# Hybrid attention and DeltaNet layer: token sums from the high and low halves, one gate block earlier, later planned output weights

## The chip, the cores and the metric

The kernel runs on one core of one Trainium2 chip. The metric is the device time of one execution in microseconds (us); lower is better. The kernel before takes 763.55 us, the median of three executions between 762.99 and 765.27 us.

## The reference, cut to what matters

One decoder layer on 512 tokens and 16 meta tokens in front of them (528 columns), width 1024. The tokens are normalised once; two branches, softmax attention (8 heads, names `a*`) and a gated DeltaNet (8 heads, names `d*`), read the same normalised tokens `hn`:

```python
hn = rms_norm(h, norm_w)
proj = hn @ w_in                     # aq ak av az dq dk dv dz db da ga gd
y_a = (rms(o_a) * 0.8 * silu(az)) @ w_branch_attn
y_d = (rms(o_d) * silu(dz)) @ w_branch_delta
merged = sigmoid(ga) * y_a + sigmoid(gd) * y_d
out = rms_norm(h + merged @ w_out, final_norm_w)[:, 16:]
```

## The kernel before, in words

**Products.** Every weight block (128 output channels, 1024 inputs) is split into a high part `wh` (rounded, by an ACT copy) and a low part `wl` (the rest, by a DVE subtraction); the tokens likewise into `hnH` and `hnL`. A product is three passes, high by high, high by low, low by high, over 8 input blocks. The blocks come in the order that `dense_order` (L34) writes out: for each of four groups of two heads, `dk` and `dv` of both heads, then `dq`, `dz` and the attention blocks, then the gates and the two branch outputs.

**Pairs.** Some neighbouring blocks (from group 0: `ak` with `av`) are computed two at a time by seven half products instead of eight (`pair_of_blocks`, L1844, the products p1 to p7 in the order p1, p2, p6, p5, p7, p4, p3). p1 and p2 read `hnH` and `hnL` directly; p6, p5, p7 and p4 read four token sums t1 to t4: sums and differences of the quarters of `hn` (512 input channels by 264 tokens, so 128 x 1056 numbers each). With the quarters called A (first channels, first tokens), B (first channels, second tokens), C and E (second channels), the kernel needs t1 = B - A, t2 = E - t1, t3 = E - B and t4 = C - t2.

**Normalising.** `normalise` (L524) squares, scales and transposes a tile of 128 tokens through PE into a PSUM bank of the kind `pat`. `part` (L557) copies the bank to `hnH` on ACT, subtracts on DVE to `hnL`, and a third task, `whole` (L563), copies the unsplit numbers on ACT into `whole_`, four SBUF tiles that are the same memory as `room0` to `room3`. The bank is given back when both `hnL` and `whole` are through. There are 12 such ACT copies.

**The sums.** `token_sums` (L607) waits for the 12 copies and for the event `ap` (L828, the end of the chain of small decay operations of `gates`, L640), then forms the four sums, one DVE subtraction each; `high_low` (L611) splits each into `sumH` (ACT) and `sumL` (DVE). When all four are split, the two `th` buffers become free, which are halves of `room3` (L835).

**Gates.** `after_gate` (L911) takes the finished product of a `dz` or `az` block out of its PSUM bank: it waits for a `th` buffer, then runs a tanh on ACT and a multiplication on DVE, and only then gives the bank back. Banks of the kind `pd`, which all dense products use, are three (L66); a pair needs one for p1 and p6, one for p2, later others.

**What sets the order of work.** All instructions are laid out before the run by a planner (`Plan`). It resumes tasks one by one: of all tasks that wait for an engine it takes the one that can start earliest by its own cost estimates, and the lower rank where two could start at the same time. Ranks: 0 for loads, splits of weights and the DeltaNet, 0.6 for `gates`, 1 for what follows a product, 2 for attention, 3 for `token_sums`, 4 for the dense products. Each engine then runs its instructions in exactly that order, so one that waits holds all behind it. `Engine.time` (L235) holds the costs; a transfer is taken to land by `transfer` (L138):

```python
self.hwdge = max(begin + 600, self.hwdge) + 460
self.dma = max(self.dma, self.hwdge) + nbytes / 360 + 20
self.arrival = self.dma + 900
```

(nanoseconds and bytes; `late`, L134, adds to the arrival). Weights come through four `raw` buffers (`load_weights`, L476, all on SP's queue, in the order of the blocks) and are split by `split` (L401). The eight blocks of `w_out` follow the last weights; numbers 4 and 5 of them are split into free `W` buffers, the others into the memory of `hn` once that is free.

**The end.** In the last pair of the attention branch (`pair_products`, L1766) PE's products p1, p6 and p7 are each followed by a copy of their bank on ACT (`snap`, L1770, tile `sn`). p4 goes on accumulating in the bank that p7 left, so PE starts it only after the copy.

All instructions are issued through one helper, so the profile's line is L231 for nearly all; the tiles tell them apart.

Of the kernel before, what the change touches and what calls it, by code (L numbers as in the profile page):

```python
# [10 lines left out]
F32 = mybir.dt.float32  # L11
# [3 lines left out]
ALU = mybir.AluOpType  # L15
# [5 lines left out]
KB = D // P  # L21
# [12 lines left out]
def dense_order():  # L34

    order = []
    for g in range(H // 2):
        k, v, q, z = ([(n, 2 * g), (n, 2 * g + 1)] for n in ("dk", "dv", "dq", "dz"))
        a0, a1 = ([(n, 2 * g + i) for n in ("ak", "av", "aq", "az")] for i in range(2))
        order += k + v + (a0 + q + z[:1] if g else q + z[:1] + a0) + a1 + z[1:]  # L40
    order += [("gd", c) for c in range(KB)] + [("ga", 0)]
    for n in range(KB):
        order += [("ga", n + 1)] * (n < KB - 1) + [(("yd", "ya")[n // 4], 2 * (n % 4) + i) for i in range(2)]
    return order
# [17 lines left out]
HALF = L // 2  # L62
# [6 lines left out]
PE, DVE, ACT, POOL, SP = "PE", "DVE", "ACT", "POOL", "SP"  # L69
# [19 lines left out]
class Plan:  # L89
# [24 lines left out]
    def spawn(self, gen, rank=None):  # L114
        time, src = self.here() if self.task else (0.0, SP)
        self.tasks.append(Task(gen, self.task.rank if rank is None else rank, time, src))
# [99 lines left out]
class Engine:  # L216
# [18 lines left out]
    def time(self, op, args, kw):  # L235
        if op == "dma_start":
            return {SP: 60, ACT: 700, POOL: 1050}[self.name]
        out = kw["out"] if "out" in kw else args[0]
        ins = [a for a in list(args[1:]) + list(kw.values()) if hasattr(a, "dtype") and hasattr(a, "space")]
        n = int(np.prod(out.shape[1:]))  # L240
        if self.name == PE:
            if op == "transpose":
                return 2 * max(n / 2.4, 53)
            dt = ins[-1].dtype
            if dt == F32:
                small = ins[0].shape[0] <= 64
                return 2 * max(2 * n / 2.4 + 4, 32 if small else 107)
            if dt == F32R:
                return n / 2.4 + (11 if n < 400 else 18) if n >= 256 else max(2 * n / 2.4, 107)
            return n / 2.4 + 57  # L250
        psum = any(a.space == PSUM for a in ins)
        if op == "tensor_reduce":
            n = int(np.prod(ins[-1].shape[1:]))
        scalar = any(hasattr(kw.get(k), "space") for k in ("scalar", "scalar1", "scale", "bias"))
        if self.name == ACT:
            return (51 if op == "copy" and psum else 94) + n / 1.2 + 50 * scalar + 93 * ("accum_out" in kw)
        if self.name == DVE:
            one = op in ("tensor_copy", "tensor_scalar", "tensor_scalar_mul", "tensor_scalar_add", "memset")
            return 69 + 60 * (scalar or op == "scalar_tensor_tensor") + n / (1.92 if one and not psum else 0.96)
        if op == "tensor_tensor":  # L260
            return 300 + 164 * n if kw["op"] == ALU.pow else 100 + 2.2 * n
        return 100 + n / 1.1
# [3 lines left out]
def hybrid_block(ctx: ExitStack, tc: tile.TileContext, x, meta, wblk, wbd, wout, pcol, prow, out):  # L266
    nc = tc.nc
    plan = Plan({**SLOTS, "wo": 0, "th": 0}, BANKS, ALL_BANKS)
    T, V, A, G, S = (Engine(plan, n, e) for n, e in
                     ((PE, nc.tensor), (DVE, nc.vector), (ACT, nc.scalar), (POOL, nc.gpsimd), (SP, nc.sync)))  # L270
    spawn, done = plan.spawn, plan.done
# [29 lines left out]
    def give(kind, at=None):  # L301
        plan.give(kind, names_.index(at.tensor.name) if kind in BANKS else 0)
# [9 lines left out]
    def tick(event, n):  # L312
        ticks[event] = ticks.get(event, 0) + 1
        if ticks[event] == n:
            done(event)
        return ticks[event] == n
# [159 lines left out]
    def load_weights(n):  # L476
        yield ("raw",)
        which = plan.task.slot
        raw = raws[which]
        yield SP  # L480
        m = n - len(ORDER)
        S.dma_start(out=raw, in_=wblk[n] if m < 0 else wout[m // 4, :, m % 4 * D:m % 4 * D + D])
        if n in PAIRED or m < 0 and ORDER[n][0] in ("yd", "ya"):
            first.append((raw, which))
            if len(first) == 2:
                spawn(split_pair(n - 1, tuple(first)), 0)
                first.clear()
        else:
            spawn(split(n, raw, which), 0.3 if n < 2 else 0 if m < 0 else 2)
# [32 lines left out]
    hn = [hnp.tile([P, KB, L], F32R, tag=t, name=t) for t in ("hnH", "hnL")]  # L522

    def normalise(n):  # L524

        yield f"x{n}"
        w = P if n == 0 else D
        ss, rs, dg = (mk(sp, [P, k], F32, t, 3) for k, t in ((1, "ss"), (1, "rs"), (P, "dg")))
        yield ACT
        A.activation(out=st[:, :w], in_=xt[n], func=AF.Square, accum_out=ss)  # L530

        def weigh():
            yield "nwb"
            yield DVE
            V.tensor_tensor(out=xt[n], in0=xt[n], in1=mt[:, P:2 * P] if n == 0 else nwb, op=ALU.mult)
            done(f"xw{n}")

        spawn(weigh())
        src = ss
        if n == 0:  # L540
            yield "same"
            yield ("pdl",)
            yield PE
            pt = bank("pdl")
            T.matmul(pt[:, 0:1], samb.rearrange("p k t -> p (k t)"), ss, start=True, stop=True)
            src = pt[:, 0:1]
        yield DVE
        V.tensor_scalar(out=ss, in0=src, scalar1=1.0 / D, scalar2=EPS, op0=ALU.mult, op1=ALU.add)
        if n == 0:
            give("pdl", pt)  # L550
        yield POOL
        G.tensor_tensor(out=rs, in0=ss, in1=mhalf[:, 0:1], op=ALU.pow)
        yield DVE
        V.tensor_scalar_mul(out=dg, in0=ident, scalar1=rs)
        yield f"xw{n}"

        def part(pt, dst):  # L557
            yield ACT
            A.copy(out=hn[0][dst], in_=pt)
            tick(f"hh{n}", 1 if n == 0 else 2)  # L560
            bank_ = f"hn bank {n} {dst[1].start}"

            def whole():  # L563

                t0, t1 = dst[2].start, dst[2].stop
                for c in (0, KB // 2) if n == 0 else (dst[1].start,):
                    for m in range(2):
                        lo, hi = max(t0, HALF * m), min(t1, HALF * m + HALF)
                        if lo < hi:
                            yield ACT  # L570
                            A.copy(out=whole_[2 * (c // 4) + m][:, :, lo - HALF * m:hi - HALF * m],
                                   in_=pt[:, c - dst[1].start:c - dst[1].start + 4, lo - t0:hi - t0])
                if tick(bank_, 2):
                    give("pat", pt)
                tick("whole", 9)

            spawn(whole(), 0.6)
            yield DVE
            V.tensor_tensor(out=hn[1][dst], in0=pt, in1=hn[0][dst].bitcast(F32), op=ALU.subtract)
            if tick(bank_, 2):  # L580
                give("pat", pt)
            tick(f"hn{n}", 1 if n == 0 else 2)

        for hf in range(1 if n == 0 else 2):
            yield ("pat",)
            yield PE
            pt = bank("pat")
            if n == 0:
                T.matmul(pt[:, 0:P], xt[0], dg, start=True, stop=True)
                pt = pt[:, 0:P].rearrange("p (k t) -> p k t", t=NM)  # L590
                dst = (slice(None), slice(0, KB), slice(0, NM))
            else:
                pt = pt.rearrange("p (k t) -> p k t", t=P)
                for k in range(4):
                    T.matmul(pt[:, k, :], xt[n][:, (4 * hf + k) * P:(4 * hf + k + 1) * P], dg, start=True, stop=True)
                dst = (slice(None), slice(4 * hf, 4 * hf + 4), slice(NM + P * (n - 1), NM + P * n))
            spawn(part(pt, dst))
# [7 lines left out]
    of_sum = dict(t1=0, t2=3, t3=1, t4=2)  # L605

    def token_sums():  # L607
        yield "whole"
        yield "ap"

        def high_low(key):  # L611
            n = of_sum[key]
            yield ACT
            A.copy(out=ts_h[n], in_=whole_[n])
            yield DVE
            V.tensor_tensor(out=ts_l[n], in0=whole_[n], in1=ts_h[n].bitcast(F32), op=ALU.subtract)
            done(key)
            if tick("sums", 4):
                for n in range(SLOTS["th"]):
                    plan.give("th", n)  # L620

        for key, (x_, y_) in dict(t1=(1, 0), t3=(3, 1), t2=(3, 0), t4=(2, 3)).items():
            yield DVE
            V.tensor_tensor(out=whole_[of_sum[key]], in0=whole_[x_], in1=whole_[y_], op=ALU.subtract)
            spawn(high_low(key))


    FULL = [(0, 272), (272, 256)]
# [1576 lines left out]
```

## Time and profile before

| | |
|---|---|
| median of 3 executions | 763.55 us (762.99 to 765.27) |
| profiled execution, own time | 767.75 us |
| its span, first to last instruction | 766.0 us |
| PE (matmul) busy | 740.0 us, 97% of the span |
| DVE busy | 620.2 us, 81% |
| ACT busy | 500.4 us, 65% |
| POOL busy | 89.6 us, 12% |
| granted TensorE clock, mean | 0.989 of full speed |

PE is TensorE's matmuls, PEld its weight loads, DVE VectorE, ACT ScalarE, POOL GpSimd, SP the engine that issues the DMAs. A row of the timeline is start, duration (us), engine, operation, output <- inputs, shapes, count, and in brackets the engine's idle time before it and what ended it. PEclk is the granted TensorE clock as a share of full speed: 1.00 is 2.4 GHz, 0.50 is 1.2 GHz.

### The profile page before, as it was taken

To read this page: it belongs to the slowest core of one execution; us is meant where nothing else is said; L and a number is where in the kernel's file an instruction comes from. 1 tells how busy PE (TensorE), PEld (TensorE's weight loads), DVE (VectorE), ACT (ScalarE), POOL (GpSimd) and SP (SyncE) were. 2 spreads that over 40 slices of the span, in tenths; PEclk is the share of its full clock that TensorE was granted. 3 is DMA by queue.
4 is the path that set the end of the run, shared out by engine and by line. 5 is a ranking of instruction groups with operands and counts; after the bars stand their busy time and mean duration, and the time that the engine had idled before them with its cause. 6 is when DMAs were issued, how large, how long until landed. Compare 5 with 4: busy or idle time off the path is not lost.

```text
span 766.0 us, 14381 instructions
## 1 busy us (share of the span) xinstructions
PE 740.0 (97%) x5311; PEld 671.6 (88%) x5311; DVE 620.2 (81%) x1427; ACT 500.4 (65%) x1318; POOL 89.6 (12%) x102
## 2 busy tenths in 40 slices
PE   4999999999999999999999999999999999999996
PEld 4998888899999799999889989988888998898775
DVE  6799999699899659989877979975697879797353
ACT  6479576679865848986587977667776446454132
POOL 4134002112000201401020311000100000000001
PEclk9999999999999979999999999999999999999999
DMA  8031423224304103421320441360123442143502
GB/s 320 30 113 32 135 83 70 70 70 149 98 33 145 31 34 119 147 81 42 118 64 22 159 135 33 120 184 30 56 83 116 147 148 91 57 131 111 193 1 110
DMA packets 45430, 74.86 MB, mean 98 GB/s; under 512 B 20728, under 2 KB 25636, under 8 KB 45360
## 3 DMA queue, kind: packets, MB, share of 16 engines
q1 hardware_dynamic: 45360, 73.95, 30.0%
q8 instruction: 41, 0.67, 0.3%
q14 instruction: 29, 0.24, 0.1%
HBM read 67.58 MB, written 6.36 MB: 97 GB/s over the span
## 4 chain that ended last, share of the span: by engine, by line
PE 74%; DVE 10%; ACT 10%; issue 2%; DMA 1%; POOL 1%; SPq 0%; POOLq 0%; DVEq 0%; ACTq 0%
PE bank L231 71%; PE psc L231 3%; ACT wh L231 2%; DVE wl L231 2%; DVE y L231 1%; ACT TM L231 1%; DMA xt<-in_x_dram 1%; POOL km L231 1%; ACT ak L231 1%; ACT e L231 1%; DMA raw<-in_wout_dram 1%; ACT ktd L231 1%; DVE ak L231 1%; DVE ast L231 1%; ACT y L231 1%
## 5 line engine op out<-in xcount | busy, mean ns | idle before, releaser
L231 PE MATMUL bank<-hnH,wh 128*128 128x512 f32 (+4 forms) x664 | 233.6, 355 | 1.6 <-ACT hnH L231 1.3
L231 PE MATMUL bank<-hnL,wh 128*128 128x512 f32 (+4 forms) x664 | 222.0, 337 | 0.0
L231 PE MATMUL bank<-hnH,wl 128*128 128x512 f32 (+4 forms) x664 | 221.7, 337 | 0.0
L231 DVE TENSOR_TENSOR wl<-raw,wh 128x1024 fp32r<-128x1024 f32 (+1 forms) x120 | 134.4, 1121 | 20.2 <-ACT wh L231 19.6
L231 ACT CAST wh<-raw 128x1024 fp32r<-128x1024 f32 (+1 forms) x120 | 116.4, 970 | 48.6 <-PE bank L231 34.5
L231 PEld LDWEIGHTS bank<-hnH,wh 128*128 128x128 f32 x664 | 124.5, 189 | 14.5 <-ACT hnH L231 1.5
L231 PEld LDWEIGHTS bank<-hnH,wl 128*128 128x128 f32 x664 | 124.3, 189 | 14.0
L231 PEld LDWEIGHTS bank<-hnL,wh 128*128 128x128 f32 x664 | 124.5, 189 | 9.5
L231 PE MATMUL bank<-sumH,wh 128*128 128x264 f32 x224 | 68.0, 303 | 0.0
L231 PE MATMUL bank<-sumL,wh 128*128 128x264 f32 x224 | 63.9, 285 | 0.4 <-DVE sumL L231 0.4
L231 PE MATMUL bank<-sumH,wl 128*128 128x264 f32 x224 | 63.8, 285 | 0.0
L231 DVE SCALAR_TENSOR_TENSOR y<-xp,pc,y 128x528 f32<-128x528 f32 (+1 forms) x72 | 54.1, 757 | 0.5 <-ACT y L231 0.5
L231 ACT ACTIVATE e<-psc,ast 128x144 f32<-128x144 f32 (+3 forms) x64 | 34.7, 542 | 18.4 <-DVE ast L231 16.6
L231 PEld LDWEIGHTS bank<-sumL,wh 128*128 128x128 f32 x224 | 42.6, 190 | 0.6 <-DVE sumL L231 0.6
L231 PEld LDWEIGHTS bank<-sumH,wh 128*128 128x128 f32 x224 | 42.7, 190 | 0.2
L231 PEld LDWEIGHTS bank<-sumH,wl 128*128 128x128 f32 x224 | 42.4, 189 | 0.0
L231 PE MATMUL bank<-btH,wh 128*128 128x256 f32 x128 | 36.2, 283 | 2.1 <-ACT sn L231 2.1
L231 PE MATMUL bank<-btH,wl 128*128 128x256 f32 x128 | 36.0, 281 | 0.0
L231 PE MATMUL bank<-btL,wh 128*128 128x256 f32 x128 | 35.9, 281 | 0.0
L231 POOL TENSOR_TENSOR ass<-ass,mhalf 128x4 f32<-128x4 f32 x8 | 10.3, 1288 | 186.8 <-DVE ass L231 175.2
L231 PE MATMUL psc<-ak,aq 128*128 128x264 f32 (+3 forms) x160 | 29.1, 303 | 0.4 <-ACT e L231 0.3
L231 DVE TENSOR_REDUCE ast<-psc 128x1 f32<-128x528 f32 (+3 forms) x40 | 28.5, 714 | 0.5
(370 smaller groups left out, 1738.2 us busy)
## 6 DMA issues: line engine op xcount, KB each, us to landing
raw<-in_wblk_dram SPq DMA_DIRECT2D x96, 512.0 KB, 3.6
raw<-in_wout_dram SPq DMA_DIRECT2D x8, 512.0 KB, 4.9
xt<-in_x_dram SPq DMA_DIRECT2D x4, 512.0 KB, 6.4
TM<-gcd SPq DMA_DIRECT2D x8, 256.0 KB, 5.9
xr<-in_x_dram SPq DMA_DIRECT2D x8, 256.0 KB, 6.0
out_dram<-xr SPq DMA_DIRECT2D x8, 256.0 KB, 2.1
room<-scrm SPq DMA_DIRECT2D x12, 128.0 KB, 3.5
oad<-room SPq DMA_DIRECT2D x6, 256.0 KB, 2.0
```

The source lines that it names most:

```text
L231: return real(*args, **kw)
```

## The change

- `whole` and its 12 ACT copies go; the bank of `normalise` is given back after the DVE subtraction for `hnL`.
- `token_sums` waits for `hnH` and `hnL` of all tokens instead, and adds and subtracts high and low parts: eight DVE operations of 128 x 1056 instead of four. Three of them need no `ap`; the other five come behind it. The sums keep to the four `room` tiles, in the order t1, t2, t3, t4.
- In group 0 the second gate block, `dz` of head 1, moves from the end of the group to right behind `dz` of head 0, ahead of the eight attention blocks (`ak`, `av`, `aq`, `az` of both heads). Its weight load, split, product and `after_gate` move with it. The other groups keep their order.
- The planner's cost of an fp32 matmul with at most 32 columns and at most 32 rows becomes 40 ns (64 ns before for 32 columns).
- The planner takes the loads of `w_out` to land 1600 ns later.

```diff
-        order += k + v + (a0 + q + z[:1] if g else q + z[:1] + a0) + a1 + z[1:]
+        order += k + v + (a0 + q + z[:1] + a1 + z[1:] if g else q + z + a0 + a1)
...
-                return 2 * max(2 * n / 2.4 + 4, 32 if small else 107)
+                return 2 * max(2 * n / 2.4 + 4, 32 if small else 107) if n > 32 or ins[0].shape[0] > 32 else 40
...
         S.dma_start(out=raw, in_=wblk[n] if m < 0 else wout[m // 4, :, m % 4 * D:m % 4 * D + D])
+        if m >= 0:
+            plan.late(1600)
...
             A.copy(out=hn[0][dst], in_=pt)
             tick(f"hh{n}", 1 if n == 0 else 2)
-            bank_ = f"hn bank {n} {dst[1].start}"
-            def whole():
...
-                            yield ACT
-                            A.copy(out=whole_[2 * (c // 4) + m][:, :, lo - HALF * m:hi - HALF * m],
-                                   in_=pt[:, c - dst[1].start:c - dst[1].start + 4, lo - t0:hi - t0])
...
-            spawn(whole(), 0.6)
             yield DVE
             V.tensor_tensor(out=hn[1][dst], in0=pt, in1=hn[0][dst].bitcast(F32), op=ALU.subtract)
-            if tick(bank_, 2):
-                give("pat", pt)
+            give("pat", pt)
...
     def token_sums():
-        yield "whole"
-        yield "ap"
+        for e in range(5):
+            yield f"hn{e}"
+        def part(c, m, j):
+            return hn[j][:, KB // 2 * c:KB // 2 * c + KB // 2, HALF * m:HALF * m + HALF].bitcast(F32)
...
-        for key, (x_, y_) in dict(t1=(1, 0), t3=(3, 1), t2=(3, 0), t4=(2, 3)).items():
-            yield DVE
-            V.tensor_tensor(out=whole_[of_sum[key]], in0=whole_[x_], in1=whole_[y_], op=ALU.subtract)
-            spawn(high_low(key))
+        t1, t3, t4, t2 = whole_
+        for key, out, x_, y_, op in (("", t4, part(0, 1, 0), part(0, 1, 1), ALU.add), ("", t3, part(1, 1, 0), part(1, 1, 1), ALU.add),
+                                     ("", t1, t4, part(0, 0, 0), ALU.subtract), ("t1", t1, t1, part(0, 0, 1), ALU.subtract),
+                                     ("t2", t2, t3, t1, ALU.subtract), ("t3", t3, t3, t4, ALU.subtract),
+                                     ("", t4, part(1, 0, 0), t2, ALU.subtract), ("t4", t4, t4, part(1, 0, 1), ALU.add)):
+            if key == "t1":
+                yield "ap"
+            yield DVE
+            V.tensor_tensor(out=out, in0=x_, in1=y_, op=op)
+            if key:
+                spawn(high_low(key))
```

## Rows read from the trace of the kernel before

**Rows 1.** Part 1 of the page: busy time, share of the span, instructions

```profile
PE 740.0 (97%) x5311; PEld 671.6 (88%) x5311; DVE 620.2 (81%) x1427; ACT 500.4 (65%) x1318; POOL 89.6 (12%) x102
```

**Rows 2.** Busy time by stretch: length, each engine (instructions), PEclk, DMA share, GB/s

```profile
12.00:24.00 12.00, 8.23 (x64) 7.41 (x64) 11.87 (x25) 10.94 (x27) 7.15 (x7) 1.00 0.67 251
24.00:46.00 22.00, 22.00 (x182) 20.89 (x181) 16.19 (x63) 7.85 (x21) 0.55 (x1) 1.00 0.16 55
46.00:84.00 38.00, 36.06 (x274) 33.50 (x274) 36.65 (x66) 31.17 (x91) 14.96 (x9) 1.00 0.23 67
...
120.00:706.00 586.00, 582.12 (x4302) 530.10 (x4301) 491.95 (x1123) 408.61 (x1106) 59.29 (x66) 0.99 0.29 91
```

**Rows 3.** Whom PE waited for, 6 to 30 us: total us, times, longest

```profile
PE bank L231 <- DVE ss L231: 1.5, 1, 1.5
PE bank L231 <- ACT hnH L231: 1.3, 1, 1.3
PE bank L231 <- ACT room L231: 0.9, 1, 0.9
```

**Rows 4.** Operations on the tile room; the first by stretch, busy us of ACT alone

```profile
8.00:26.00 18.00, 0.00 (x0) 0.00 (x0) 0.00 (x0) 5.47 (x12) 1.00 0.68 261
...
L231 DVE TENSOR_TENSOR room<-room,room x4: 1239/1240/1241, 46.3 to 59.8; 128x1056 f32<-128x1056 f32 x4
```

**Rows 5.** Timeline of DVE: one of the last hnL of normalising, two gaps after it

```profile
22.89 0.68 DVE L231 TENSOR_TENSOR hnL<-bank,hnH 128x512 fp32r<-128x512 f32 x1
...
28.41 0.41 DVE L231 COPY bdT<-bank 32x256 f32<-32x256 f32 x1 [1.97 <-PE bank L231]
...
37.01 0.19 DVE L231 COPY gc<-bank 128x32 f32<-128x32 f32 x1 [1.94 <-PE bank L231]
```

**Rows 6.** Timeline of PE, 75 to 82 us

```profile
75.70 0.40 PE L231 MATMUL bank<-hnH,wl 128*128 128x512 f32 x1
75.94 0.28 PE L231 MATMUL bank<-hnH,wh 128*128 128x264 f32 x1
...
78.72 0.28 PE L231 MATMUL bank<-hnH,wl 128*128 128x264 f32 x1
79.87 1.16 PE L231 MATMUL bank<-qT,kT 128*128 128x128 f32 x8 [0.86 <-DVE qT L231]
...
81.98 0.39 PE L231 MATMUL bank<-sumL,wh 128*128 128x264 f32 x1 [0.39 <-DVE sumL L231]
```

**Rows 7.** Timeline of DVE and of ACT, 82 to 85 us

```profile
82.45 1.23 DVE L231 TENSOR_TENSOR sumL<-room,sumH 128x1056 fp32r<-128x1056 f32 x1
...
84.54 0.69 DVE L231 SCALAR_TENSOR_TENSOR room<-room,bank 128x512 f32<-128x512 f32 x1 [0.16 <-ACT room L231]
...
83.90 0.61 ACT L231 ACTIVATE room<-bank 128x512 f32<-128x512 f32 x1
```

**Rows 8.** Timeline of SP, ACT and PE near the end

```profile
703.99 4.49 SPq L231 DMA_DIRECT2D raw<-in_wout_dram  x4
...
708.95 1.04 ACT L231 CAST wh<-raw 128x1024 fp32r<-128x1024 f32 x1 [2.86 <-DMA raw<-in_wout_dram]
709.90 0.36 ACT L231 COPY sn<-bank 128x256 f32<-128x256 f32 x1
...
707.91 0.28 PE L231 MATMUL bank<-btH,wl 128*128 128x256 f32 x1
710.32 0.39 PE L231 MATMUL bank<-btH,wh 128*128 128x256 f32 x1 [2.12 <-ACT sn L231]
```

**Rows 9.** Busy time by stretch, columns as in rows 2, where the granted clock fell

```profile
265.00:268.00 3.00, 1.84 (x20) 1.59 (x18) 1.47 (x3) 2.79 (x7) 0.00 (x0) 1.00 0.37 131
268.00:278.20 10.20, 10.20 (x60) 9.04 (x59) 5.52 (x12) 2.05 (x7) 0.00 (x0) 0.50 0.18 66
...
712.00:714.00 2.00, 2.00 (x11) 2.00 (x11) 1.38 (x3) 0.00 (x0) 0.00 (x0) 0.50 0.72 172
714.00:716.00 2.00, 2.00 (x10) 1.73 (x9) 1.29 (x3) 0.23 (x1) 0.00 (x0) 0.71 0.87 167
```

More of the change, by code (lines that the diff above doesn't have):

```diff
@@ L560, in part @@
             tick(f"hh{n}", 1 if n == 0 else 2)
-            bank_ = f"hn bank {n} {dst[1].start}"
-            def whole():
[L565 to L569, printed above, removed]
-                            yield ACT
-                            A.copy(out=whole_[2 * (c // 4) + m][:, :, lo - HALF * m:hi - HALF * m],
-                                   in_=pt[:, c - dst[1].start:c - dst[1].start + 4, lo - t0:hi - t0])
-                if tick(bank_, 2):
-                    give("pat", pt)
-                tick("whole", 9)
-            spawn(whole(), 0.6)
             yield DVE
             V.tensor_tensor(out=hn[1][dst], in0=pt, in1=hn[0][dst].bitcast(F32), op=ALU.subtract)
-            if tick(bank_, 2):
-                give("pat", pt)
+            give("pat", pt)
             tick(f"hn{n}", 1 if n == 0 else 2)
```

## The prediction

> **What bounds the kernel now.** I read the page's busy times first: PE is busy for 740.0 of 766.0 us, DVE for 620.2, ACT for 500.4 [rows 1]. So PE sets the end, and an edit is worth what PE's idle time and PE's half-speed time change by. Then the busy times by stretch [rows 2]. From 12 to 24 us PE works 8.23 of 12 us while DVE (11.87) and ACT (10.94) are nearly full: normalising holds PE. From 24 to 46 PE is full and DVE has 5.8 us free. From 46 to 84 DVE is busy 36.65 of 38 us and PE loses 1.9. From 120 to 706 PE loses 3.9 us in 586: little to win there. At the start PE waits 1.5 us for DVE, 1.3 for an `hnH` copy and 0.9 for an ACT copy into room [rows 3], together 3.7. In the timeline of 75 to 82 us PE waits 0.86 for a DVE product of the DeltaNet, and 0.39 for `sumL` [rows 6]. Near the end there is one stall of 2.12 us [rows 8]. Last, the clock: PE runs at 0.50 for 10.2 us from 268, and again for some 3 us around 713 [rows 9].
>
> The sum is made against the profiled execution, 767.75 us with a span of 766.0 (1.75 lie around it). It is 4.2 above the median of 763.55. The clock drop at 268 can cost up to half of its 10.2 us, 5.1, so the likeliest reading is that most executions lack that one. I take the difference over to the median and count nothing for this drop.
>
> **Start: the 12 ACT copies go.** They are 5.47 us of ACT up to 26 us [rows 4], in a stretch where ACT is full. With them go the waits of `hnH` behind them and the second condition for the `pat` bank: at most all 3.7 us of PE's waits [rows 3]. But DVE does the same weighing, weight splits and `hnL` as before and is full [rows 2], and the 1.5 us wait is for DVE itself. At least 0 is won. I take half, -1.9 us, since 0.9 + 1.3 stand against ACT and 1.5 against DVE. The last `hnL` then end earlier than now (one of them runs at 22.89, [rows 5]).
>
> **The sums: eight DVE operations for four.** One takes 1.24 us [rows 4], so DVE gains 4 x 1.24 = 5.0 us. Three need no `ap` and become ready when the last `hnL` is done. The planner puts them, rank 3 or not, into the first gaps of DVE, and there are gaps of 1.97 and 1.94 us at 28 and 37, where DVE waits for PE [rows 5], in 5.8 us free. Cost on PE: 0, hidden by the dense products, which keep PE full until 46 [rows 2]; if they push the chain of small gate operations back, each by up to 1.24, `ap` moves by as much, again beside dense products. Five stand behind `ap` where four stood: 1.24 us more in a stretch with 38 - 36.65 = 1.35 free. So the last sum, whose low half runs now from 82.45 to 83.68 [rows 7], ends about 1.2 later, less what the earlier start gives back.
>
> **The moved gate block.** Its load (one DMA on SP's queue, which passes those of the eight attention blocks, each of them one place later), its two split operations, its 24 matmuls and its tanh and multiplication all move ahead. 24 matmuls of 512 columns at 0.24 us spacing [rows 6] give PE 5.6 us of work that needs no sum before the first pair. The 0.39 us wait for `sumL` goes: -0.4. The 0.86 us wait is of another chain and stays. But the gate needs a `th` buffer, these come free only when all four sums are split, and until then a finished `dz` keeps its `pd` bank. Now one `dz` waits there; after the change two of three banks wait. p1 takes the third, and p2 has none. What the bank waits for is priced so. Now p1 begins at 75.94; it would begin 5.6 + 0.86 + 1.6 us later (the DeltaNet's products at 79.87 to 81.46 and the wait before them come first): 84.0. p1 and p2 are 24 matmuls in 2.9 us [rows 6], so p1 ends at 85.5. The sums end at 83.68 + 1.24 = 84.9, and from the end of the sums to the end of the first gate (tanh at 83.90, multiplication 84.54 to 85.23, [rows 7]) it is 1.55 us: 86.5. PE waits 1.0 us if PE and DVE both start earlier, and 1.0 + 1.9 = 2.9 if only PE does. Below, 0: the pair's own splits come later too and leave DVE to the sums. I take 2.0, the middle of 1.0 and 2.9, as DVE has little room to move. Together +1.6, bounds -0.4 and +2.5.
>
> **The cost of small matmuls.** No instruction changes; only the planner's clock runs ahead by less in the DeltaNet. Worth 0; bounds the 3.9 us that PE loses from 120 to 706 [rows 2] on one side, and as much again on the other, since another order has other waits.
>
> **The output weights.** At 703.99 SP issues the load of the fifth block; ACT's copy of it starts at 708.95, after 2.86 us of waiting for the data, and behind it stands the copy `sn` (709.90, 0.36 us) on which PE waits [rows 8]. PE had finished that bank at 707.91 + 0.28 = 708.19. By its code the planner expects the data 600 + 460 + 1456 + 20 + 900 = 3436 ns after the issue, at 707.4 on this clock; it took 4.96. So it thought the weight copy ready 0.8 us before `sn`. With 1600 more the data stand at 709.0, behind `sn`, and the two copies change places. PE then goes on 0.5 us after 708.19 (0.36 for the copy, 0.06 from its end to PE as now, as much before it) instead of 2.12: -1.6. Who is late next: the weight copy itself, by 0.4 us, for weights first used after 740. If the planner keeps the order: 0.
>
> **The clock behind that stall.** Behind it the clock is 0.50 from 712 to 714 and 0.71 in the mean to 716 [rows 9]: 2 x 0.50 + 2 x 0.29 = 1.6 us of full-speed work lost. With 0.5 us of idle time in place of 2.12 I expect no drop and take -1.5, bounds 0 and -1.6. The rows alone do not make this sure: idle gaps of 1.3 to 1.5 us at the start were followed by no drop [rows 2, 3], and 1.2 us before 267 [rows 9] was. [...]
>
> **Sum.** -1.9 + 1.6 - 1.6 - 1.5 = -3.4 us: 763.55 - 3.4 = 760.1.
>
> **The rivals.**
> *The start is lost again in the DVE-bound stretch, and the clock term was never in the median.* For it: DVE busy 36.65 of 38 us. Against it: PE is full from 24 to 46 and gets 5.6 us of free work. The start's -1.9 is given back in waits between 46 and 90, the tail gives -1.6 and no more: 763.55 - 1.6 = 762.0, no change. [...] Chance 0.28.
> *Two gates hold the banks and the clock falls.* The wait for the bank reaches its 2.9 us bound; as after the gaps of 1.2 and 2.12 us, PE's clock falls for the next 10.2 us, 5.1 lost. It decides once the wait is over 1.2 us. -1.9 - 0.4 + 2.9 + 5.1 - 3.1 = +2.6: 766.2, slower. Against it: 0.86 at 79 us caused no drop. Chance 0.16.
> *Everything comes through.* All 3.7 us of the start, no wait for banks (-0.4), the tail (-3.1): -7.2, 756.4. For it: ACT stands before two of the three waits. Against it: DVE is full in that stretch. Chance 0.14.
> *The planner's order does not flip at the end* (the change does not do what it says there): only -1.9 + 1.6 = -0.3, 763.3. Against it: 1.6 us stands against a lead of 0.8. Chance 0.06.
>
> **How the numbers follow.** A measurement of this kernel can tell 0.3%, 2.3 us, from no change: the borders are 761.3 and 765.8. The forecast has 0.36, most of it below 761.3 (0.30), the rest (0.06) within. The lost start is within (0.24) or below (0.04); the banks with the clock are above (0.11) or within (0.05); everything through is below; the unflipped order is within. That gives 0.48 faster, 0.41 the same, 0.11 slower. The range reaches down to 755.5, just below the case in which all comes through, and up to 766.5, just above the slower rival; beyond lie about 2 in 10, the other ends of the 3.9 us from 120 to 706.
>
> **What would show each step.** Right: no ACT copy into room before 30 us and PE idle less than 2.5 us between 12 and 20; three additions of 128 x 1056 on DVE before 46 us and five after; the second `dz` ahead of the first pair; a wait of PE for a gate's bank near 85 us, of 1 to 3 us; at the end `sn` ahead of the weight copy, an idle time of PE near 0.5 us, and a granted clock of 1.00 through it. Wrong: as many waits at the start as before; a clock drop between 80 and 130; the stall before `sn` still above 1.5 us; or losses between 120 and 706 that differ from 3.9 by more than 2 us, which none of my steps would explain.

## The result, and the profile after

The changed kernel takes 757.24 us, the median of 6 executions (757.21 to 758.72). The kernel before, timed beside it, takes 763.27 (760.65 to 765.27, 6 executions). The ratio is 0.9927 [0.9902, 0.9952]: faster by 6.0 us in the medians. The forecast was 760.1, 3.4 us faster.

The medians hide a difference of kind. The executions of the kernel before spread over 8 us, and for the most part they spread with the clock: of 29 timed beside the first experiments, those of 760.4 to 761.3 us have a mean granted clock of 0.997 to 0.999, those of 765.1 to 765.6 one of 0.991 to 0.993, and the four of 767.6 to 768.2 one of 0.989. Five of the six executions of the changed kernel lie between 757.21 and 757.25, at 0.997 to 0.999. Fastest against fastest the gain is 760.43 - 757.21 = 3.2 us. How much of the other 2.8 is clock is not settled: at one and the same mean clock of 0.997 nine of the 29 executions lie between 760.43 and 763.54, the median one (763.04) among them, and the six that were timed beside the changed kernel have no clock on record. The profiled execution of the changed kernel has an own time of 757.23, a span of 755.5 and a clock of 0.998.

The profile of the changed kernel, part 1 of the page, answers to [rows 1]. PE has 6 us less of busy time, as it ran less at half speed; DVE has 4.3 us more and ACT 4.6 us less:

```profile
PE 734.0 (97%) x5311; PEld 666.7 (88%) x5311; DVE 624.5 (83%) x1431; ACT 495.8 (66%) x1306; POOL 84.4 (11%) x102
```

Busy time by stretch, columns as in [rows 2]. From 12 to 24 us PE works 9.95 us in place of 8.23. From 24 to 46 DVE works 20.70 in place of 16.19 and PE stays full. From 46 to 84 PE works 0.3 more. From 120 to 706 PE is idle for 3.4 us in place of 3.9. In the last two rows the clock is 1.00 where [rows 9] had it at 0.50:

```profile
12.00:24.00 12.00, 9.95 (x77) 9.03 (x76) 11.97 (x22) 7.29 (x15) 7.02 (x7) 1.00 0.71 254
24.00:46.00 22.00, 22.00 (x185) 21.29 (x184) 20.70 (x67) 9.29 (x20) 1.14 (x2) 1.00 0.14 50
46.00:84.00 38.00, 36.34 (x261) 33.27 (x260) 35.69 (x68) 29.22 (x85) 14.81 (x8) 1.00 0.21 61
...
120.00:706.00 586.00, 582.62 (x4338) 530.61 (x4337) 498.88 (x1141) 410.03 (x1108) 53.80 (x66) 1.00 0.31 95
...
268.00:278.20 10.20, 10.01 (x93) 9.29 (x94) 8.05 (x19) 7.11 (x20) 1.01 (x1) 1.00 0.17 53
...
712.00:716.00 4.00, 4.00 (x20) 3.26 (x19) 0.00 (x0) 0.00 (x0) 0.00 (x0) 1.00 0.14 48
```

Whom PE waited for from 6 to 30 us, columns as in [rows 3]: 2.1 us in place of 3.7, and no wait for a copy into room:

```profile
PE bank L231 <- DVE ss L231: 1.3, 2, 0.9
PE bank L231 <- ACT hnH L231: 0.8, 1, 0.8
```

Timeline of DVE: the first of the three early operations (the others start at 28.03 and 29.53), the first of the five behind `ap` (the last starts at 58.27), the last `sumL`, and the multiplication of the first gate:

```profile
26.79 1.24 DVE L231 TENSOR_TENSOR room<-hnH,hnL 128x1056 f32<-128x1056 f32 x1
...
49.64 1.24 DVE L231 TENSOR_TENSOR room<-room,hnL 128x1056 f32<-128x1056 f32 x1
...
82.67 1.25 DVE L231 TENSOR_TENSOR sumL<-room,sumH 128x1056 fp32r<-128x1056 f32 x1
...
85.04 0.68 DVE L231 SCALAR_TENSOR_TENSOR room<-room,bank 128x512 f32<-128x512 f32 x1
```

Timeline of PE, to be held against [rows 6] and, for its last row, [rows 8]. The waits of 0.86 for `qT` and 0.39 for `sumL` are gone. p2 begins at 83.03, p6 at 84.58, neither with a wait. A new wait of 1.66 us stands at 70.36. The stall near the end is 0.46 in place of 2.12:

```profile
70.36 0.28 PE L231 MATMUL bank<-ident,vm 128*32 128x128 f32 x1 [1.66 <-POOL vm L231]
...
81.68 1.16 PE L231 MATMUL bank<-qT,kT 128*128 128x128 f32 x8
...
83.03 0.37 PE L231 MATMUL bank<-hnH,wh 128*128 128x264 f32 x1
...
701.33 0.38 PE L231 MATMUL bank<-btH,wh 128*128 128x256 f32 x1 [0.46 <-ACT sn L231]
```

There the two copies on ACT have changed places, as the timeline of ACT shows (in [rows 8] `wh` came first):

```profile
700.91 0.37 ACT L231 COPY sn<-bank 128x256 f32<-128x256 f32 x1 [2.14 <-PE bank L231]
701.17 1.05 ACT L231 CAST wh<-raw 128x1024 fp32r<-128x1024 f32 x1
```

The new wait has its cause on POOL. Timeline of POOL before it:

```profile
61.61 7.95 POOL L231 TENSOR_TENSOR ms<-ms,phalf 32x1 f32<-32x1 f32 x1 [2.45 <-DVE ms L231]
69.53 0.63 POOL L231 TENSOR_SCALAR_AFFINE_SELECT TM<-TM 128x512 f32<-128x512 f32 x1
70.12 0.19 POOL L231 COPY vm<-y 128x16 f32<-128x16 f32 x1
```

and of DVE at its end:

```profile
68.41 0.73 DVE L231 SCALAR_TENSOR_TENSOR y<-xp,pc,y 128x512 f32<-128x512 f32 x1
70.20 0.35 DVE L231 SCALAR_TENSOR_TENSOR MT<-bank,sc,TM 128x128 f32<-128x128 f32 x1 [1.05 <-POOL TM L231]
```

A power of 32 numbers takes 7.95 us (3.74 in the kernel before), and the copy `vm` stands behind it. From its start to 69.14 DVE runs without a gap, most of the time in operations with two inputs in SBUF (`y`, `sumL`, `wl`, `raw`); then DVE itself has to wait for POOL, and the power ends at 69.56, 0.42 us into that pause. The tile that `vm` copies was written by DVE at 67.19 for 0.69 us. So the copy could have run at 67.9 and PE lost its 1.66 us for POOL.

That it is DVE's unbroken run which holds the power up, and not the power itself, the traces of all fourteen kernels here, those of the next section included, show together: in eleven of them this power takes 1.68 to 7.95 us, and in each of the eleven it ends 0.40 to 0.42 us after the start of DVE's first pause of 0.1 us or more; in the other three it takes 0.55 us in all.

### The profile page after: what moved, and what is told of

It is laid out like the page before. It is cut to its first block, busy times and chain, and to the rows that moved or that the text cites. A ratio compares the mean times of both kernels' runs of the same rounds, so it can differ in the third digit from the quotient of the medians.

```text
span 755.5 us, 14375 instructions
## 1 busy us (share of the span) xinstructions
PE 734.0 (97%) x5311; PEld 666.7 (88%) x5311; DVE 624.5 (83%) x1431; ACT 495.8 (66%) x1306; POOL 84.4 (11%) x102
## 4 chain that ended last, share of the span: by engine, by line
PE 81%; DVE 7%; ACT 5%; issue 2%; POOL 2%; DMA 1%; SPq 0%; POOLq 0%; ACTq 0%; DVEq 0%
PE bank L231 78%; PE psc L231 3%; DVE wl L231 2%; DVE y L231 1%; ACT wh L231 1%; POOL ms L231 1%; DMA xt<-in_x_dram 1%; ACT ak L231 1%; ACT sqk L231 0%; DVE aq L231 0%; DMA odd<-room 0%; ACT TM L231 0%; DVE room L231 0%; DVE hnL L231 0%; POOL ass L231 0%
## 5 line engine op out<-in xcount | busy, mean ns | idle before, releaser
L231 PEld LDWEIGHTS bank<-hnH,wh 128*128 128x128 f32 x664 | 124.4, 189 | 14.7 <-ACT hnH L231 1.0
L231 ACT CAST wh<-st 128x1024 fp32r<-128x1024 f32 x22 | 23.1, 1048 | 16.2 <-PE bank L231 15.9
L231 POOL TENSOR_TENSOR ass<-ass,mhalf 128x4 f32<-128x4 f32 x8 | 8.7, 1084 | 222.8 <-DVE ass L231 163.4
L231 DVE TENSOR_TENSOR wl<-st,wh 128x1024 fp32r<-128x1024 f32 x22 | 27.8, 1266 | 2.4 <-ACT wh L231 2.3
```

What stands on the lines that cost most here:

```text
L231: return real(*args, **kw)
```

## The experiments

Twelve kernels, each timed in five rounds beside the kernel before. Medians, their ranges, and the ratio to the kernel before with its 95% interval:

| kernel | median, us | ratio |
|---|---|---|
| before (67 executions beside these) | 763.04, 764.87, 763.93 in the three series | |
| changed | 757.24 (757.21 to 758.72) | 0.9927 [0.9902, 0.9952] |
| before + later output weights | 760.18 (759.87 to 764.69) | 0.9983 [0.9964, 1.0002] |
| before + sums | 762.87 (761.42 to 766.34) | 1.0002 [0.9981, 1.0023] |
| before + moved gate | 767.55 (766.14 to 770.11) | 1.0064 [1.0040, 1.0088] |
| before + price | 769.69 (768.27 to 770.65) | 1.0065 [1.0039, 1.0091] |
| changed - later output weights | 759.65 (757.89 to 761.30) | 0.9946 [0.9921, 0.9970] |
| changed - sums | 784.96 (783.43 to 787.12) | 1.0268 [1.0224, 1.0311] |
| changed - moved gate | 757.52 (757.41 to 759.27) | 0.9900 [0.9869, 0.9932] |
| changed - price | 774.09 (772.83 to 774.53) | 1.0118 [1.0077, 1.0159] |
| changed, price 36 for 40 ns | 771.96 (771.06 to 774.11) | 1.0109 [1.0067, 1.0152] |
| changed, price 44 for 40 ns | 758.93 (758.43 to 760.26) | 0.9937 [0.9912, 0.9962] |
| changed, all `vm` copies on ACT | 773.80 (772.64 to 777.91) | 1.0125 [1.0080, 1.0169] |
| changed, first group's `vm` on ACT | 776.08 (772.37 to 777.92) | 1.0147 [1.0105, 1.0190] |

"Price" is the planner's cost of a small fp32 matmul, which no instruction feels: only the order of the work follows from it.

**The output weights alone, and all but them.** The kernel before with

```diff
+        if m >= 0:
+            plan.late(1600)
```

> The kernel before with the 1600 ns on the loads of the output weights alone. My theory (a stall and the clock drop behind it): the copy sn stands ahead of the weight copy, PE's idle time there falls from 2.1 to about 0.5 us, the granted clock stays 1.00 through 708 to 716, and the time falls by 3.1 us against the kernel before in the same rounds (0.4%). Rival (the clock drop is not tied to that stall): only 1.6 us, with a stretch of half clock still near 712. Rival (nothing of the change's gain lies here): under 0.8 us.

and the changed kernel without these two lines:

> The kernel after without the 1600 ns. My theory: the stall of about 2 us before the last p4 is back with a stretch of half clock behind it, 3.1 us slower than after (760.3), the rest of the profile as after's, since nothing ahead of the output weights changes. Rival: the stall alone, 1.6 us slower (758.8), at full clock.

Measured: 760.18 alone, 759.65 without, 2.9 us below its own kernel before and 2.4 above the changed kernel; fastest against fastest only 760.43 - 759.87 = 0.6 and 757.89 - 757.21 = 0.7. Timeline of PE and busy time by stretch of the kernel with the later weights alone:

```profile
704.00 0.38 PE L231 MATMUL bank<-btH,wh 128*128 128x256 f32 x1 [0.46 <-ACT sn L231]
```

```profile
265.00:267.00 2.00, 0.83 (x8) 0.62 (x5) 0.83 (x2) 1.96 (x6) 0.00 (x0) 1.00 0.27 37
268.00:278.20 10.20, 10.17 (x98) 9.45 (x97) 7.29 (x20) 5.74 (x23) 1.01 (x1) 1.00 0.19 61
```

and of the changed kernel without them:

```profile
704.42 0.38 PE L231 MATMUL bank<-btH,wh 128*128 128x256 f32 x1 [1.92 <-ACT sn L231]
```

```profile
18.10:21.50 3.40, 3.40 (x17) 3.40 (x18) 2.85 (x3) 1.06 (x2) 3.29 (x3) 0.50 0.60 187
...
712.00:716.00 4.00, 4.00 (x20) 3.26 (x19) 0.00 (x0) 0.00 (x0) 0.00 (x0) 1.00 0.84 321
```

So the wait changes in both as forecast: 0.46 for 1.92 to 2.12. In time the edit alone is not clear of no change (its interval reaches 1.0002), and a fall of the clock does not follow such a stall each time. The idle time at 265 us (1.17 of 2.00 us) is followed by a clock of 1.00 here, by 0.50 in [rows 9]; the stall of 1.92 at 704 is followed by 1.00 here, the one of 2.12 in [rows 8] by 0.50; and this time it is a stall of 0.83 us at 18 us that has 3.4 us at 0.50 behind it, where one of 0.91 in the changed kernel has none. Why the fastest executions differ by 0.6 to 0.7 and not by the stall's 1.5 to 1.7 is open: of the two kernels that have the long stall no fast execution is profiled, so how long it is there is not shown.

**The sums alone.** The kernel before with the new `token_sums` and without `whole`:

```diff
-            spawn(whole(), 0.6)
...
-        yield "whole"
-        yield "ap"
+        for e in range(5):
+            yield f"hn{e}"
...
+            if key == "t1":
+                yield "ap"
```

> The kernel before with the new token sums alone (no ACT copies, eight DVE operations), old order, old planner costs. My theory: PE's waits between 12 and 20 us fall from 3.7 to about 2, half of what the copies could give back, and 1.5 to 2 us reach the end; the last sum ends about 1 us later than 83.7. Rival (DVE is full from 46 to 84, the start is lost there again): waits shorter at the start, longer between 46 and 90, time within 0.8 us of before. A gain of over 4 us would say that something else than the start is won, such as the half-clock stretch at 268.

Measured: 762.87, the same as the kernel before; its fastest, 761.42, is 1.0 above the fastest of that. The start is the changed kernel's: PE's waits from 6 to 30 us are 1.2 and 0.8. But the timeline of PE has

```profile
80.88 0.59 PE L231 MATMUL bank<-sumL,wh 128*128 128x264 f32 x1 [3.82 <-DVE sumL L231]
```

and the busy time by stretch shows the clock that follows it:

```profile
80.50:83.90 3.40, 3.02 (x14) 3.02 (x15) 3.40 (x6) 0.00 (x0) 0.00 (x0) 0.50 0.38 124
```

The start's gain comes as forecast and is given back in the stretch where DVE is full: what the first rival said.

**The moved gate alone.** The kernel before with

```diff
-        order += k + v + (a0 + q + z[:1] if g else q + z[:1] + a0) + a1 + z[1:]
+        order += k + v + (a0 + q + z[:1] + a1 + z[1:] if g else q + z + a0 + a1)
```

> The kernel before with the second gate block of group 0 moved alone. My theory as predicted, corrected by the profile of after (no wait for a bank there): the 0.4 us wait for sumL goes and nothing else, time within 1 us of before unless the half-clock stretch at 268 goes too (then up to 3 us less in the median). Rival (the moved block carries the gain): 2 us or more less with the waits of PE between 60 and 90 us under 1 us. Rival (two gates hold the banks): a wait of 1 us or more for a gate's bank near 80 us.

Measured: 767.55, slower. No wait for a gate's bank, and none for `sumL`; the timeline of PE has 3.24 us for `vm`, that of POOL what comes before it:

```profile
72.00 0.28 PE L231 MATMUL bank<-ident,vm 128*32 128x128 f32 x1 [3.24 <-POOL vm L231]
```

```profile
57.86 8.13 POOL L231 TENSOR_TENSOR sc<-sc,phalf 128x4 f32<-128x4 f32 x1 [5.19 <-DVE sc L231]
...
71.75 0.20 POOL L231 COPY vm<-y 128x16 f32<-128x16 f32 x1 [3.04 <-DVE y L231]
```

Again a power of a few numbers takes 8 us (it ends 0.89 us after DVE's run does, which pauses from 65.10 to 66.92), but here POOL was idle for 3.04 us ahead of the copy: DVE was late with `y`. The wait bears the same name as the changed kernel's and has another cause.

**All but the moved gate.** The changed kernel with the old line of the order.

> The changed kernel with the first group's second gate back behind its heads. Theory (the moved gate pays for the later sums: its products need no sum and cover them): PE waits for sumL again near 77 us, 3 to 5 us in one piece as with the sums alone, and the time is 760.5 to 762. Rival (the long wait of the kernel with the sums alone came from the planner's too high price of the small matmuls, which this kernel has corrected): no wait above 1 us for sumL, and 757 to 758.5.

Measured: 757.52, and PE's timeline has

```profile
80.17 0.39 PE L231 MATMUL bank<-sumL,wh 128*128 128x264 f32 x1 [0.95 <-DVE sumL L231]
...
82.56 1.16 PE L231 MATMUL bank<-qT,kT 128*128 128x128 f32 x8 [0.79 <-DVE qT L231]
```

The rival holds: with the price corrected the sums need no cover. The moved gate is worth 0.3 us in the changed kernel, less than what another order alone can move (1.7, below at 44 ns). The waits of 0.95 and 0.79 return without it, and the wait for `vm` falls from 1.66 to 0.46.

**All but the sums.** The changed kernel with `whole` and the four sums of before.

> The changed kernel with ACT's copies of unsplit tokens and the four sums of before. Theory (the sums' own edit gives the 1.7 us at the start, and the moved gate works by itself once the planner prices small matmuls right): 758.5 to 759.5, PE's loss in the first 20 us back at about 6.7, no wait for POOL above 2 us. Rival (the moved gate without the new sums brings DeltaNet work ahead and PE waits for POOL's copy vm, as with the order alone): a wait of PE of about 3.4 us for vm near 68 us, and 761 to 764.

Measured: 784.96, 27.7 us above the changed kernel, beyond both expectations. The start is that of [rows 3] again (1.5, 1.3 and 0.8), and the wait for `vm` is there. Most of the rest is neither. Whom PE waited for, 46 to 120 us and then 100 to 740 us:

```profile
PE bank L231 <- POOL vm L231: 3.1, 1, 3.1
...
PE bank L231 <- DVE vT L231: 6.0, 3, 3.5
PE bank L231 <- DVE kT L231: 3.1, 2, 1.7
PE bank L231 <- ACT ao L231: 1.9, 1, 1.9
```

**All but the price.** The changed kernel with

```diff
-                return 2 * max(2 * n / 2.4 + 4, 32 if small else 107) if n > 32 or ins[0].shape[0] > 32 else 40
+                return 2 * max(2 * n / 2.4 + 4, 32 if small else 107)
```

> The changed kernel with the planner's old price for the small matmuls. Theory (the price is worth nothing, as forecast): 756.8 to 757.8, the same waits of PE between 46 and 90 within 0.5 us. Rival (the order of DeltaNet work beside the sums depends on it): another order between 60 and 90 us with a wait of PE of 2 us or more for POOL's vm or for sumL, and 759 to 763.

Measured: 774.09, 16.9 us above the changed kernel. Neither theory had it: the stretch from 46 to 90 us has one wait, 1.4 us for `vm`, as in the changed kernel; the loss comes after 340 us. Whom PE waited for, 100 to 740 us:

```profile
PE bank L231 <- DVE vT L231: 4.9, 3, 3.4
PE bank L231 <- ACT ao L231: 1.8, 1, 1.8
```

The longest is in PE's timeline at 497.75. Ahead of it DVE's timeline ends a long chain of dependent operations `tmps` and `ts`, and only then come the two `vT` that PE waits for:

```profile
497.75 0.59 PE L231 MATMUL bank<-hnH,wh 128*128 128x264 f32 x1 [3.39 <-DVE vT L231]
```

```profile
487.44 0.24 DVE L231 TENSOR_TENSOR tmps<-room,ts 99x91 f32<-99x91 f32 x1
...
497.18 0.17 DVE L231 TENSOR_TENSOR ts<-ts,tmps 99x11 f32<-99x11 f32 x1
497.27 0.76 DVE L231 TENSOR_TENSOR vT<-bank,cn 128x264 f32<-128x264 f32 x2
```

In the changed kernel the same two `vT` (the last of sixteen such operations) stand in the middle of that chain (its operation of 99 x 91 is at 484.00, its last but one at 496.70), and PE has no wait there:

```profile
486.66 0.43 DVE L231 TENSOR_TENSOR vT<-bank,cn 128x264 f32<-128x264 f32 x1
...
487.76 0.42 DVE L231 TENSOR_TENSOR vT<-bank,cn 128x264 f32<-128x264 f32 x1
...
496.70 0.17 DVE L231 TENSOR_TENSOR tmps<-room,ts 99x11 f32<-99x11 f32 x1
```

The wait also costs clock; busy time by stretch of the kernel without the price, behind the waits for `ao` and `vT`:

```profile
365.00:370.00 5.00, 4.73 (x19) 4.54 (x20) 2.56 (x7) 1.04 (x1) 2.06 (x4) 0.50 0.53 150
...
497.70:502.00 4.30, 4.25 (x18) 4.16 (x19) 1.44 (x3) 1.63 (x5) 0.40 (x2) 0.50 0.35 48
```

**The price alone.** The kernel before with the new line.

> The kernel before with the planner's new price for the small matmuls alone. Theory (the price decides the order of the DeltaNet work and by that is worth many us, but which way depends on the other edits): over 2 us from the kernel before in one direction or the other, with other waits of PE between 120 and 560 us. Rival (the price is worth nothing where the other edits are missing, as forecast): within 1 us of the kernel before, losses of PE from 120 to 706 within 2 us of its own.

Measured: 769.69, 5.8 us slower than the kernel before in the same rounds. The largest of PE's waits from 100 to 740 us are 3.9 us in two pieces for `ao` and 1.5 for `kT`. The theory holds: the same line is worth -16.9 us beside the other edits and +5.8 without them.

**The price off by 4 ns.** The changed kernel with 36 and with 44 in place of 40.

```diff
-... > 32 else 40
+... > 32 else 36
```

> The changed kernel with a planner's price of 36 ns in place of 40 for the small matmuls, which no instruction's duration depends on. Theory (the time hangs on the particular order that the plan falls into, and a price 4 ns off falls into another): 759 to 772, with waits of PE for vT, kT, ao or tdmt in 200 to 560 us that the changed kernel doesn't have. Rival (a price near the right one gives a good order, the old one a bad one): 756.5 to 758.5.

> The changed kernel with a planner's price of 44 ns in place of 40. Theory (the particular order decides): 759 to 772, and another sum of waits than at 36. Rival (near the right price the order is good): 756.5 to 758.5, as at 36.

Measured: 771.96 and 758.93. At 36 the waits for `vT` (3.5) and `ao` (2.1) are there; at 44 the longest of PE's waits from 100 to 740 us is 0.6. At 44 the time falls between the two expectations. A price nearer the truth does not explain this: in the timeline of the kernel before twenty matmuls of 32 x 32 start between 264.18 and 264.49, 16 ns apart in the mean, so 36 is nearest of the three, and it is worse than 40 by 14.7 us, while 44 is worse by 1.7. The particular order decides.

**`vm` on ACT.** The changed kernel with all copies `vm` on ACT, and with the first group's alone:

```diff
-            yield POOL
-            G.tensor_copy(out=vm[:, 16 * i:16 * i + 16], in_=v[:, 0:NM])
+            yield ACT
+            A.copy(out=vm[:, 16 * i:16 * i + 16], in_=v[:, 0:NM])
```

> The changed kernel with the two copies vm on ACT instead of POOL, so that PE's wait of 1.66 us at 68 us no longer stands behind POOL's slow pow. Theory (POOL, held up by DVE's back to back operations, is all that this wait is): the wait goes or falls under 0.4 us, and the time is 755.5 to 756.3. Rival (something behind it is as late, DVE's chain that reads the pow first of all): a wait of over 1 us stays within 65 to 75 us under another name, and the time is within 0.4 us of 757.2 or above.

> The changed kernel with the two copies vm of the first group alone on ACT in place of POOL. Both theories agree that the wait of 1.66 us at 68 us falls under 0.5, as it did with all copies moved. Theory (the rest of the plan falls into another order): the gain of 1.3 us at 68 is lost again later, 759 to 774. Rival (all the loss with every copy moved came from the copies of the later groups): 755.3 to 756.5, faster than the changed kernel.

Measured: 773.80 and 776.08. In both the only wait of PE from 55 to 90 us is 0.2 for `qT`. In the second, ACT's copy runs at 68.45, and POOL's power of 32 numbers, now at 58.33, takes 1.68. Timelines of POOL and of DVE, which pauses from 59.60 to 59.80:

```profile
58.33 1.68 POOL L231 TENSOR_TENSOR ms<-ms,phalf 32x1 f32<-32x1 f32 x1 [0.63 <-DVE ms L231]
...
59.80 1.23 DVE L231 TENSOR_TENSOR wl<-raw,wh 128x1024 fp32r<-128x1024 f32 x1 [0.21 <-ACT wh L231]
```

So the wait of 1.66 us does go, as far as that stretch is concerned. Later PE waits again, 100 to 740 us:

```profile
PE bank L231 <- DVE vT L231: 4.2, 1, 4.2
PE bank L231 <- ACT ao L231: 3.8, 2, 1.9
```

Moving two copies of 0.2 us in the first group costs 18.8 us (15.2 fastest against fastest), by waits in the other three groups. No version here beats the changed kernel.

## Why the prediction was right, and where not

The sign and the size came out: 757.24 lies in the range, 2.9 us below the forecast, which itself was below the border of no change. Its steps fared unequally, and part of the agreement is luck: the forecast charged 2.0 us for a wait that did not come, and it put at nothing the step on which the order hangs, by which kernels next to this one take 770 us and more.

*Start, -1.9.* Right as to the waits. PE's fell from 3.7 to 2.1 us, -1.6, with the sums alone as with the whole change, and they are back with the old sums. What goes and what stays is as argued: the wait for ACT's copy is gone, the one for `hnH` is shorter, DVE's stays. Two things were not: the last `hnL` ends at 26.52, later than before (25.30) and not earlier, and the wait for ACT's copy is not there in every execution without the edit, as the comparison below shows.

*The sums, three hidden and five behind `ap`.* Right as to place: three operations before 31 us, five from 49.64 on, and PE is full from 24 to 46. Mis-sized at the end: the last `sumL` ends at 83.92, 0.24 later than in [rows 7] and not 1.2.

*The moved gate block, -0.4 + 2.0.* The wait of 2.0 us "for a bank" failed: it is 0. p2 starts at 83.03, before the first gate's multiplication at 85.04 has ended, so it waits for no gate. The three `pd` banks are the planner's count; there are six physical banks, and as p1 (from 80.12) and p2 write theirs before the two gates' multiplications (85.04 and 86.66) read theirs, these four have different ones. A count in the planner shapes the order but is no semaphore. The step also left out the wait that did come, 1.66 us for `vm`. Its size is near the 2.0 by accident. The Trainium skill's page SBUF — State Buffer (SBUF: two separate sides) says that a DVE operation with two SBUF inputs and a GpSimd operation that reads SBUF hold one pair of ports in turn, exclusively; the 7.95 us beside an unbroken run of such DVE operations agree with it. The page speaks of one instruction; here POOL was kept out until a whole run of them paused, and which of DVE's operations do that was not separated. In the changed kernel the step as a whole is worth -0.3 (757.52 against 757.24), not +1.6.

*The cost of small matmuls, "worth 0; bounds the 3.9 us".* This step failed most. Taken out of the changed kernel it costs 16.9 us, put alone into the kernel before it costs 5.8, and 4 ns less costs 14.7. The bounds were taken from what PE loses from 120 to 706 us in the order that the trace shows, with as much again for another order. A planned order can be far worse than that: a `vT` that stands at the end of a chain on DVE and not in its middle makes PE wait 3 to 4 us, and at half clock behind it for some us more, in more than one group.

*Output weights, -1.6.* The mechanism is shown: `sn` ahead of `wh`, idle time 0.46 where 0.5 was forecast, clock 1.00. The fastest executions gained 0.6 to 0.7 by it.

*Clock, -1.5 for the drop behind 712 and nothing for the one at 268.* Right for the profile, open for the median. What the two medians differ by beyond 3.2 us, 2.8, is in part clock, but the median execution of the 29 (763.04) has a clock of 0.997, as the fastest one has. The stall ahead of 268 is gone in the changed kernel's order (PE works 10.01 of 10.20 us from 268 on, and 265 to 267 is full), and five of its six executions lie within 0.04 us of each other. The Trainium skill's page TensorE: Matmul & The Clock Gate (Part 1, The HAM clock gate) calls the slow matmuls at a kernel's start run-variable, as the monitor's window is free-running. Inside this kernel the runs show the like: one kernel gave 760.4 at a clock of 0.997 and 768.2 at 0.989. The 1.2 us of wait that the second rival took for decisive are no border: the clock fell behind a stall of 0.83 us and stayed up behind one of 1.92.

The steps cannot be added up from these runs, since the kernel before was profiled in an execution of 767.75 us with two falls of the clock. A fairer pair is the kernel with the later output weights alone, profiled at 759.95, and the changed kernel at 757.23: in both the clock is 1.00 up to 740 us and the stall near the end is 0.46. Busy time by stretch of the first:

```profile
12.00:24.00 12.00, 9.10 (x65) 8.23 (x65) 11.87 (x25) 11.05 (x26) 7.15 (x7) 1.00 0.69 252
46.00:84.00 38.00, 35.98 (x274) 33.43 (x273) 36.63 (x66) 31.42 (x91) 14.72 (x9) 1.00 0.22 67
120.00:700.00 580.00, 576.05 (x4289) 524.48 (x4288) 490.15 (x1121) 407.32 (x1104) 59.27 (x66) 1.00 0.30 92
```

PE's idle time in the changed kernel is 0.85 us less from 12 to 24 us, 0.36 less from 46 to 84, and 1.04 less from 120 us to the same point near the end (2.91 of the 577.30 us to 697.30, against 3.95); PE's busy time is 0.6 less, and before 12 us it idles 0.1 more. That is the 2.7 us between them. So like with like the start gives 0.85 and not 1.6: the wait of 0.9 for ACT's copy into room is not there in this execution. And the largest term is one that the forecast put at 0: other waits from 120 us on.

That the forecast comes near says little of the edits one by one: alone on the kernel before they gave 760 to 770, left out of the changed kernel 758 to 785. The terms hold for the one order that the changed kernel has. The first rival came true for the sums alone, and the rival of two gates that hold the banks nowhere. The third, in which everything comes through, came nearest in time (756.4): no wait for a bank, a short stall and a clock of 1.00 at the end are as it said, but of the start it counted all 3.7 us.

What makes an order bad is shown only as far as the waits: in every kernel of 769 us and more PE waits longer than in the changed one for `vT` and for `ao`, and in all of these but the one without the price for `kT`. That the planner takes DVE's chain too short is likely and was not tried: by its formula an operation of 99 x 91 costs 69 + 91 / 0.96 = 164 ns, the rows have 240, and the power on POOL 464 ns against 7.95 us.

## What to carry to other kernels

Where a program lays out the order of all instructions from estimated costs, an edit's effect is its own cost plus that of falling into another order, and the second can be ten times the first: change one estimate by a tenth and time that too, before a gain or a loss is put down to the edit. Read at the engine's queue what is planned ahead of a late operation, not only which operation was late. Price a small operation on POOL by the length of the run of DVE operations that it falls into, not by its own size. And compare the fastest executions and the clock of each beside the medians: here one kernel's executions differ by 8 us, while the change is worth 3 to 6.

## What the runs showed of the hardware that was not expected

- A POOL power of 32 numbers takes 0.55 us in three of the runs and 1.68 to 7.95 us in the other eleven, where it ends 0.40 to 0.42 us after the run of DVE operations beside it first pauses. A power of 128 x 4 takes 8.13 us and ends 0.89 us after such a pause. Copies of 0.2 us on POOL are stretched too (`vm` at 51.57 takes 1.17 us in the changed kernel), there without a pause of DVE.
- TensorE's clock falls to 0.50 for 3.4 to 10.2 us, behind stalls of 0.83 to 3.8 us; behind like stalls in other executions (0.91 us at 18, 1.17 at 265, 1.92 at 704) it stayed at 1.00.
